# A hybrid encoder layer with the feed-forward layer's first product transposed: weights stationary, activations moving

## The chip, the cores and the metric

The kernel runs on one core of a Trainium2 chip. The metric is device time in microseconds for one execution; the figure is the median of several runs. The profile is one execution of its own, taken by the hardware profiler. The engines are PE (TensorE: matmuls; PEld is its loading of stationary operands), DVE (VectorE), ACT (ScalarE), POOL (GpSimd) and SP (SyncE, which issues the transfers).

## What is computed

One encoder layer with 256 rows (`S`), model width 2048 (`D`) and feed-forward width 8192 (`DFF`), in float32. The change touches the feed-forward part alone:

```python
# mod = silu(c) @ W_ada + b_ada -> shift, scale, gate of the mixer and of the FFN
h = modulate(rmsnorm(x, g_norm_ffn), shift_f, scale_f)     # (256, 2048)
f = jnp.square(jax.nn.relu(h @ w_ff1))                     # (256, 8192)
x = x + gate_f * (f @ w_ff2)                               # (256, 2048)
y = rmsnorm(x, g_final)
```

To keep float32 accuracy with the faster format fp32r, every operand is split into a rounded high part and the low remainder, and a product is the sum of three: high·high, activation high·weight low, activation low·weight high.

## The kernel before

The 256 rows are two token tiles (`T` = 2) of 128. A matmul takes a stationary operand of 128 × 128 and moves up to 512 columns past it, and its result stands in a PSUM bank of 128 × 512 floats. All big products go through `block` (L282): it fetches two k's (2 × 128 rows of weights, 1024 columns, 1 MB) at a time into a ring of `RAW_BUFS` = 5 raw tiles (DMA issued by SP), `split` (L120) casts each 128 × 1024 slice to the high part on ACT (L123) and subtracts on DVE for the low part (L124), with `W_BUFS` = 4 tiles of each. Then come the matmuls of L309: stationary is the activation slice of one k and one token tile, high or low; moving are 512 weight columns. A block of 1024 columns fills four banks, one for each token tile and column half, from the pool of four "mm" banks that all blocks share; the last two k's go token tile by token tile, and `evac` follows for each bank.

The feed-forward stage runs like this:

- `h2_first(t)` (L835) makes the modulated, normalised and transposed h of k 0 to 7 for one token tile: transposes (L858), modulation (L829, L831), high part on ACT (L863), low part on DVE (L864). `h2_first(0)` runs in the middle of the mixer's output product, `h2_first(1)` behind it.
- `ff1_first(ci)` (L904), for chunks 0 to 3 of 1024 hidden columns: the product over k 0 to 7, copied to `parts[ci]` (L906). Beside it the stream `ada_l` makes scale and shift of the FFN on DVE (L376; SP fetches 1 MB for every two of its steps). The first of these blocks takes the first 6 k's token tile by token tile (`HEAD` = 3), so that its 36 matmuls of tile 0 stand ahead of the first of tile 1.
- `h2_second` (L878), when `shift_f` is there and turned into columns by 16 matmuls (L417): h for k 8 to 15, with 16 transposes (L889), high part L892, low part L893.
- The main loop (L992): `ff1(ci)` (k 8 to 15 for the first four chunks, all 16 k's for the others), then `ff2(ci - 1)`, then `ff_T(ci)`. `ff1`'s `evac` adds the stored part on DVE, applies ReLU on ACT and squares on DVE into `rl`, which is token-major. `ff_T` (L929) turns it: 16 transposes of 128 × 128 in four banks, a copy to `fh` on ACT (L938), a subtraction to `fl` on DVE (L939). `ff2` (L942) is two blocks of 8 k's with `fh` and `fl` as stationary operands and `evac` into `acc` (L951 and on).

The order of instructions on each engine is a static list: the `run` calls interleave the generators, and a scheduler sets the list by the order and its own estimate of times. Each engine works through its list in order.

## Time and profile before

| | |
|---|---|
| median of 3 runs | 1185.48 us (1183.98 to 1187.21) |
| the profiled execution, its own time | 1184.91 us |
| its span in the trace | 1183.1 us |
| mean granted TensorE clock | 0.993 |
| PE busy | 1139.7 us, 96%, 5502 matmuls and transposes |
| DVE busy | 810.0 us, 68% |
| ACT busy | 552.4 us, 47% |
| moved by DMA | 297.50 MB, mean 251 GB/s |

The span runs from the first to the last instruction in the trace; the 1.8 us beside it are what the execution's own time has more. The feed-forward stage takes from about 448 us, the first `f1a` matmul, to the end. In rows of the timeline a line is a run of like instructions: its start, its time to the end of the last one, their number (x4), and in brackets how long the engine had been idle before and what released it. [...]

### The profile page before, as it was taken

What the parts mean: (1) busy time and instruction counts of PE and PEld (TensorE: products, weight loads), DVE (VectorE), ACT (ScalarE), POOL (GpSimd) and SP (SyncE); (2) the same over time, 40 slices, a digit from 0 to 9 for tenths busy, and PEclk for the clock granted to TensorE, in tenths of its full rate; (3) what the DMA queues carried; (4) which work ended last, traced back from release to release, by engine and by line L of the source; (5) the groups of instructions that cost most, each with busy time, mean ns of one, the idle gap of its engine ahead of it and who ended that gap; (6) DMA issues with size and microseconds to landing.
All of it is one profiled execution on the core that took longest, in us unless ns stands there. A gap on an engine that the chain in (4) does not pass through costs nothing.

```text
span 1183.1 us, 14211 instructions
## 1 busy us (share of the span) xinstructions
PE 1139.7 (96%) x5502; PEld 913.8 (77%) x5502; DVE 810.0 (68%) x1012; ACT 552.4 (47%) x811; POOL 53.3 (5%) x50
## 2 busy tenths in 40 slices
PE   5999999998999998999999999999999999999996
PEld 4566778865778886888888888888888888888875
DVE  3245559996899869775754666676686676555776
ACT  3432334547774436545545444344344344344343
POOL 1000000112101000000000000000020002000000
PEclk9999999999999999999999999999999999999999
DMA  9999974786788877995565646667868767556531
GB/s 347 393 390 369 359 302 131 258 308 215 294 307 300 300 276 275 356 329 194 184 225 179 204 158 207 232 236 263 278 220 277 280 241 249 183 181 203 183 104 72
DMA packets 94196, 297.50 MB, mean 251 GB/s; under 512 B 5712, under 2 KB 16167, under 8 KB 93488
## 3 DMA queue, kind: packets, MB, share of 16 engines
q1 hardware_dynamic: 94016, 296.56, 71.3%
q8 instruction: 43, 0.70, 0.2%
q14 instruction: 25, 0.20, 0.0%
q10 hardware_dynamic: 112, 0.03, 0.0%
HBM read 294.47 MB, written 2.10 MB: 251 GB/s over the span
## 4 chain that ended last, share of the span: by engine, by line
PE 59%; DVE 1%; issue 1%; ACT 0%; ACTq 0%; POOLq 0%; POOL 0%
PE f_p L309 51%; PE f1a_p L309 7%; PE fT L936 1%; DVE x_res L954 0%; DVE acc L953 0%; DVE acc L951 0%; PE shift_f_pc L417 0%; PE scale_f_pc L417 0%; PE h2T L889 0%; ACT acc L885 0%; DVE acc L957 0%; ACT sq L960 0%; PE h2a L858 0%; ACT h2a10t L831 0%; ACT acc L981 0%
## 5 line engine op out<-in xcount | busy, mean ns | idle before, releaser
L124 DVE TENSOR_TENSOR f_w_lo<-f_r,f_w_hi 128x1024 fp32r<-128x1024 f32 x224 | 277.2, 1245 | 200.9 <-ACT f_w_hi L123 200.8
L123 ACT CAST f_w_hi<-f_r 128x1024 fp32r<-128x1024 f32 x224 | 236.2, 1054 | 317.6 <-PE f_p L309 300.3
L309 PE MATMUL f_p<-f_w_hi,h 128*128 128x512 f32 x768 | 209.5, 391 | 0.0
L309 PEld LDWEIGHTS f_p<-f_w_hi,h 128*128 128x128 f32 x768 | 143.4, 188 | 29.3 <-ACT h L892 0.2
L309 PE MATMUL f_p<-f_w_lo,fh 128*128 128x512 f32 x512 | 158.9, 389 | 0.0
L309 PE MATMUL f_p<-f_w_hi,fh 128*128 128x512 f32 x512 | 158.5, 390 | 0.3 <-ACT fh L938 0.3
L309 PE MATMUL f_p<-f_w_hi,fl 128*128 128x512 f32 x512 | 158.7, 389 | 0.0
L309 PE MATMUL in_p<-in_w_hi,hT 128*128 128x512 f32 (+1 forms) x512 | 140.8, 388 | 4.6 <-ACT hT L364 2.8
L309 PE MATMUL f_p<-f_w_lo,h 128*128 128x512 f32 x384 | 118.9, 390 | 0.0
L309 PEld LDWEIGHTS in_p<-in_w_hi,hT 128*128 128x128 f32 x512 | 95.0, 189 | 29.0 <-ACT in_w_hi L123 6.3
L309 PEld LDWEIGHTS f_p<-f_w_hi,fh 128*128 128x128 f32 x512 | 96.0, 188 | 21.6 <-DVE acc L951 1.2
L309 PEld LDWEIGHTS f_p<-f_w_hi,fl 128*128 128x128 f32 x512 | 96.0, 188 | 20.0
L309 PEld LDWEIGHTS f_p<-f_w_lo,fh 128*128 128x128 f32 x512 | 96.1, 188 | 19.7
L124 DVE TENSOR_TENSOR in_w_lo<-in_r,in_w_hi 128x1024 fp32r<-128x1024 f32 (+1 forms) x64 | 73.2, 1169 | 45.1 <-ACT in_w_hi L123 44.9
L309 PEld LDWEIGHTS f_p<-f_w_lo,h 128*128 128x128 f32 x384 | 72.0, 188 | 14.8
L309 PE MATMUL in_p<-in_w_lo,hT 128*128 128x512 f32 (+1 forms) x256 | 78.8, 386 | 1.7 <-DVE in_w_lo L124 1.5
L123 ACT CAST in_w_hi<-in_r 128x1024 fp32r<-128x1024 f32 (+1 forms) x64 | 62.8, 1010 | 37.0 <-PE in_p L309 27.4
L309 PE MATMUL f1a_p<-f1a_w_hi,h 128*128 128x512 f32 x256 | 69.4, 391 | 3.0 <-ACT h L863 3.0
L309 PEld LDWEIGHTS f1a_p<-f1a_w_hi,h 128*128 128x128 f32 x256 | 47.8, 188 | 14.0 <-ACT h L863 3.9
L309 PEld LDWEIGHTS in_p<-in_w_lo,hT 128*128 128x128 f32 x256 | 47.7, 189 | 12.2 <-DVE in_w_lo L124 5.1
L123 ACT CAST out_w_hi<-out_r 128x1024 fp32r<-128x1024 f32 x30 | 31.6, 1052 | 35.7 <-PE out_p L309 35.7
L376 DVE SCALAR_TENSOR_TENSOR gate_f<-gate_f_r,cs,gate_f 128x1024 f32<-128x1024 f32 x32 | 40.9, 1280 | 7.0 <-DMA gate_f_r<-w_ada 6.9
(341 smaller groups left out, 1374.9 us busy)
## 6 DMA issues: line engine op xcount, KB each, us to landing
f_r<-w_ff SPq DMA_DIRECT2D x112, 1024.0 KB, 5.6
in_r<-w_in SPq DMA_DIRECT2D x24, 1024.0 KB, 9.9
sc__r<-w_ada SPq DMA_DIRECT2D x16, 1024.0 KB, 12.1
sh__r<-w_ada SPq DMA_DIRECT2D x16, 1024.0 KB, 13.4
gate_m_r<-w_ada SPq DMA_DIRECT2D x16, 1024.0 KB, 6.8
scale_f_r<-w_ada SPq DMA_DIRECT2D x16, 1024.0 KB, 8.0
...
```

What stands on the lines that cost most here:

```text
L123: s.copy(hi, src)
L124: v.tensor_tensor(lo, src, hi.bitcast(F32), ALU.subtract)
L309: pe.matmul(ps[t][j][:, 0:nw], lhsT=lhs[(lk0 + kk) // 8][:, (lk0 + kk) % 8, t * P:(t + 1) * P], rhs=rhs[:, n0:n0 + nw], start=(kk == 0 and ...
L376: v.scalar_tensor_tensor(acc, raw[:, i, :], cs[:, k + i:k + i + 1], acc, op0=ALU.mult, op1=ALU.add)
L936: pe.transpose(pt[:, i * S + t * P:i * S + (t + 1) * P], rl[:, t, (kp + i) * P:(kp + i + 1) * P], ident)
```

## The change

`ff1` is turned round. `ff1_block` (L901 to L944 of the new file) handles 512 hidden columns (`SC`; 16 blocks, numbered `si`) in four banks `u` of 128 hidden columns each. The stationary operand is now a 128 × 128 weight slice; moving are activations. h's high and low parts lie side by side in one tile (`both`), so a high weight goes against [h high | h low], 512 columns, and fills both halves of a bank; a low weight goes against h high, 256 columns, and adds to the left half. A raw tile holds four k's of 512 columns. The last four k's go bank by bank, each followed by its `evac`. The bank's two halves are then added: for `f1a` a copy of the left half on ACT and an addition on DVE into `parts`; for the first eight `ff1` blocks two DVE additions (stored part, then right half); for the other eight a copy on ACT and an addition. For each pair of banks a `scalar_tensor_tensor` on DVE takes max with 0 and multiplies by itself, ACT casts the high part of f and DVE subtracts for the low part, both straight into a tile `fs[si]`, hidden-major, as `ff2` needs it. `ff_T` goes.

The first `f1a` block (`by_tile`) loads all its weights, then takes the high weights against token tile 0 (32 matmuls of 2 × 128 columns), against token tile 1, and then the low weights against both tiles. `HEAD` goes from `block`.

`ff2(ci)` takes `fs[2ci]` and `fs[2ci + 1]`, uses other banks ("at" and "gv"), and comes after `ff1(2ci + 2)`, so one `ff1` block stands between it and the last f that it needs; the last `ff2` follows the last `ff1`. The gate's stream starts at `si` = 8. The other edits only lay out tiles.

```diff
-    def block(w_view, k0, nk, c0, w, lhs_hi, lhs_lo, name, evac, lk0=None, tail=1, rot=0, head=1, mid=None):
+    def block(w_view, k0, nk, c0, w, lhs_hi, lhs_lo, name, evac, lk0=None, tail=1, rot=0, mid=None, kdiv=8, tags=("mm",) * 4):
...
-                ps = [[bank(f"{name}_p{t}{j}", "mm") for j in range(2)] for t in range(T)]
+                ps = [[bank(f"{name}_p{t}{j}", tags[2 * t + j]) for j in range(2)] for t in range(T)]
...
-            if not last and (k + 2 + 2 * tail > nk or k + 2 < 2 * head):
+            if not last and k + 2 + 2 * tail > nk:
...
-            outer = last or k + 2 == 2 * head > 2
-            order = [(t, e) for t in range(T) for e in held] if outer else [(t, e) for e in held for t in range(T)]
+            order = [(t, e) for t in range(T) for e in held] if last else [(t, e) for e in held for t in range(T)]
...
-                pe.matmul(ps[t][j][:, 0:nw], lhsT=lhs[(lk0 + kk) // 8][:, (lk0 + kk) % 8, t * P:(t + 1) * P],
+                pe.matmul(ps[t][j][:, 0:nw], lhsT=lhs[(lk0 + kk) // kdiv][:, (lk0 + kk) % kdiv, t * P:(t + 1) * P],
...
-    def pair(name, halves, dt=F32R):
-        return [[act.tile([P, 8, S], dt, tag=f"h{hf}{part}", name=f"{name}{hf}{part}") for hf in halves]
-                for part in range(2)]
+    def both(name, hf):
+        return act.tile([P, 8, 2, S], F32R, tag=f"h{hf}", name=f"{name}{hf}")
+
+    def pair(name, halves):
+        tiles = [both(name, hf) for hf in halves]
+        return [[t_[:, :, part, :] for t_ in tiles] for part in range(2)]
...
-            v.tensor_tensor(h2_lo[0][:, 4 * q:4 * q + 4, tl], t3, hq.bitcast(F32), ALU.subtract)
+            v.tensor_tensor(h2[0][:, 4 * q:4 * q + 4, 1, tl], t3, hq.bitcast(F32), ALU.subtract)
...
-            s.copy(h2_hi[1][:, k - 8, :], tmp)
-            v.tensor_tensor(h2_lo[1][:, k - 8, :], tmp, h2_hi[1][:, k - 8, :].bitcast(F32), ALU.subtract)
+            s.copy(h2[1][:, k - 8, 0, :], tmp)
+            v.tensor_tensor(h2[1][:, k - 8, 1, :], tmp, h2[1][:, k - 8, 0, :].bitcast(F32), ALU.subtract)
...
+    SC = 512
+    NS = DFF // SC
+    NU = SC // P
+
+    def ff1_block(si, k0, nk, name, evac, by_tile=False):
+        ps, held = None, []
+        for k in range(0, nk, 4):
+            raw = raw_tile([P, 4, SC], f"{name}_r{k}")
+            sy.dma_start(raw, w_ff1_v[:, k0 + k:k0 + k + 4, si * SC:(si + 1) * SC])
+            for i in range(0, 4, 2):
+                hi, lo = split([P, 2, SC], raw[:, i:i + 2, :], f"{name}_w{k + i}")
+                held += [(k + i + j, hi[:, j, :], lo[:, j, :]) for j in range(2)]
+            if ps is None:
+                ps = [bank(f"{name}_p{u}", "mm") for u in range(NU)]
+            last = k + 4 >= nk
+            if by_tile and not last:
+                yield 0.0
+                continue
+
+            def mm(u, w, kk, o, h, start, stop):
+                pe.matmul(o, lhsT=w[:, u * P:(u + 1) * P], rhs=h, start=start, stop=stop)
+
+            def act_of(kk):
+                return h2[(k0 + kk) // 8][:, (k0 + kk) % 8]
+
+            if by_tile:
+                for t in range(T):
+                    tl = slice(t * P, (t + 1) * P)
+                    for u in range(NU):
+                        for kk, hi, lo in held:
+                            mm(u, hi, kk, ps[u].rearrange("p (a q) -> p a q", a=2)[:, :, tl], act_of(kk)[:, :, tl],
+                               t == 0 and kk == 0, False)
+                for u in range(NU):
+                    for kk, hi, lo in held:
+                        mm(u, lo, kk, ps[u][:, 0:S], act_of(kk)[:, 0, :], False, kk == nk - 1)
+                    evac(u, ps[u])
+            else:
+                order = [(u, e) for u in range(NU) for e in held] if last else [(u, e) for e in held for u in range(NU)]
+                for u, (kk, hi, lo) in order:
+                    h = act_of(kk)
+                    if kk == nk - 1:
+                        mm(u, lo, kk, ps[u][:, 0:S], h[:, 0, :], False, False)
+                        mm(u, hi, kk, ps[u], h.rearrange("p a q -> p (a q)"), False, True)
+                        evac(u, ps[u])
+                    else:
+                        mm(u, hi, kk, ps[u], h.rearrange("p a q -> p (a q)"), kk == 0, False)
+                        mm(u, lo, kk, ps[u][:, 0:S], h[:, 0, :], False, False)
+            yield 2.6 * len(held) * SC / 1024
+            held = []
+
+    def ff1_first(si):
+        def evac(u, ps):
+            part = parts[si // 2][:, si % 2 * NU + u, :]
+            s.copy(part, ps[:, 0:S])
+            v.tensor_tensor(part, ps[:, S:2 * S], part, ALU.add)
+
+        yield from ff1_block(si, 0, 8, f"f1a_{si}", evac, by_tile=si == 0)
+
+    fs = {}
+
+    def ff1(si):
+        split_k = si < 8
+        pool, tag = ((act, "n0"), (act, "n1"), (ff, "rl"))[si % 3]
+        f = fs[si] = pool.tile([P, 2, NU, S], F32R, tag=tag, name=f"f{si}")
+        box = []
+
+        def evac(u, ps):
+            if u % 2 == 0:
+                box[:] = [small.tile([P, 2, S], F32, tag="tmp", name=f"fr{si}{u}", bufs=2)]
+            tmp = box[0]
+            tu = tmp[:, u % 2, :]
             if split_k:
+                v.tensor_tensor(tu, ps[:, 0:S], parts[si // 2][:, si % 2 * NU + u, :], ALU.add)
             else:
+                s.copy(tu, ps[:, 0:S])
+            v.tensor_tensor(tu, ps[:, S:2 * S], tu, ALU.add)
+            if u % 2:
+                us = slice(u - 1, u + 1)
+                v.scalar_tensor_tensor(tmp, tmp, 0.0, tmp, op0=ALU.max, op1=ALU.mult)
+                s.copy(f[:, 0, us, :], tmp)
+                v.tensor_tensor(f[:, 1, us, :], tmp, f[:, 0, us, :].bitcast(F32), ALU.subtract)
 
         k0 = 8 if split_k else 0
+        yield from ff1_block(si, k0, KT - k0, f"f1_{si}", evac)
...
-    def ff2(ci, f_hi, f_lo, last):
+    def ff2(ci, last):
...
+            f_hi, f_lo = ([fs[2 * ci + i][:, part] for i in range(2)] for part in range(2))
...
+                             tail=TAIL[1] if last and n0 else 1, kdiv=NU, tags=("at", "at", "at", "gv"))
...
-    run((42.0, chain(*[ff1_first(ci) for ci in range(NSPLIT)])), (LW, ada_l))
+    run((42.0, chain(*[ff1_first(si) for si in range(8)])), (LW, ada_l))
     if late:
         run((1.0, flush()))
     h2_second()
-    pend = None
-    for ci in range(NCH + 1):
-        hold = []
-        if ci == NSPLIT and ada_f is None:
+    gate_f, ada_f = None, None
+    for si in range(NS + 1):
+        if si == 8:
             gate_f = act.tile([P, D], F32, tag="gate", name="gate_f")
             ada_f = chain(ada_gate(5, gate_f, "gate_f", late), flush())
-        na = 0 if ada_f is None or ci == 0 else 3 if NSPLIT == 4 else 2
-        if ci < NCH:
-            run((42.0, ff1(ci, hold)), (2.0, take(ada_f, na)))
-        if pend is not None:
-            last = ci == NCH
-            run((42.0, ff2(ci - 1, *pend, last)), (2.0, take(ada_f, na)))
-        if ci < NCH:
-            pend = ff_T(ci, hold[0])
-        if ci == 5:
+        if si < NS:
+            run((21.0, ff1(si)), (2.0, take(ada_f, 2 if ada_f else 0)))
+        if si >= 2 and si % 2 == 0:
+            run((42.0, ff2(si // 2 - 1, si == NS)), (2.0, take(ada_f, 3 if ada_f else 0)))
+        if si == 11:
             gfin = ff.tile([P, D], F32, tag="gfin", name="gfin")
             sy.dma_start(gfin, g_final.partition_broadcast(P))
 
```

PE, at the start of the first `f1a` block, before: `f1a_p` are banks, `h_3695` and `h_3696` the high and low part of h for k 0 to 7, `h2a` the transposes of token tile 1. The two rows of tile 0 with the transposes between them:

```order
L309 MATMUL f1a_p_3831<-f1a_w_hi,h_3695 128x512
L309 MATMUL f1a_p_3830<-f1a_w_lo,h_3695 128x512
L858 MATMUL h2a_3781<-ident,xs_3778 128x128 x4
L858 MATMUL h2a_3793<-ident,xs_3778 128x128 x4
L309 MATMUL f1a_p_3831<-f1a_w_lo,h_3695 128x512
L309 MATMUL f1a_p_3830<-f1a_w_hi,h_3696 128x512
```

Of the change, from the block's first matmul: four banks (3823 to 3826) of tile 0, eight k's each, high weights alone, then the transposes, then the same for tile 1, then the low weights.

```order
L917 MATMUL f1a_p_3823<-h_3690,f1a_w_hi 128x2x128 x4
L917 MATMUL f1a_p_3824<-h_3690,f1a_w_hi 128x2x128
L917 MATMUL f1a_p_3823<-h_3690,f1a_w_hi 128x2x128 x4
L917 MATMUL f1a_p_3824<-h_3690,f1a_w_hi 128x2x128 x7
L917 MATMUL f1a_p_3825<-h_3690,f1a_w_hi 128x2x128 x8
L917 MATMUL f1a_p_3826<-h_3690,f1a_w_hi 128x2x128 x8
L858 MATMUL h2a_3775<-ident,xs_3772 128x128 x4
L858 MATMUL h2a_3787<-ident,xs_3772 128x128 x4
L917 MATMUL f1a_p_3823<-h_3690,f1a_w_hi 128x2x128 x8
L917 MATMUL f1a_p_3824<-h_3690,f1a_w_hi 128x2x128 x8
L917 MATMUL f1a_p_3825<-h_3690,f1a_w_hi 128x2x128 x8
L917 MATMUL f1a_p_3826<-h_3690,f1a_w_hi 128x2x128 x8
```

The low weights have moved behind tile 1's matmuls, and 32 matmuls stand ahead of tile 1's.

DVE, where `h2_second` starts, before: `mf` are the modulation's columns, `h2t` the modulated h of one k, `h_3808` the low part of h for k 8 to 15.

```order
L423 COPY mf<-shift_f_pc 128x8
L829 TENSOR_SCALAR h2t_4477<-h2T_4474,mf 128x256
L124 TENSOR_TENSOR f_0_w_lo<-f_0_r_4568,f_0_w_hi 128x1024
L893 TENSOR_TENSOR h_3808<-h2t_4477,h_3807 128x256
L893 TENSOR_TENSOR h_3808<-h2t_4484,h_3807 128x256
L829 TENSOR_SCALAR h2t_4491<-h2T_4488,mf 128x256
L893 TENSOR_TENSOR h_3808<-h2t_4491,h_3807 128x256
L893 TENSOR_TENSOR h_3808<-h2t_4498,h_3807 128x256
```

Of the change, from the same copy; `part` and `f1a_p` belong to the last `f1a` block's `evac`, `f_0_w_lo` to the splits of the first `ff1` block.

```order
L421 COPY mf<-shift_f_pc 128x8
L123 TENSOR_TENSOR f_0_w_lo<-f_0_r_4796,f_0_w_hi 128x1024
L951 TENSOR_TENSOR part_3810<-f1a_p_4592,part_3810 128x256
L831 TENSOR_SCALAR h2t_4696<-h2T_4693,mf 128x256
L123 TENSOR_TENSOR f_0_w_lo<-f_0_r_4796,f_0_w_hi 128x1024
L891 TENSOR_TENSOR h_3801<-h2t_4696,h_3801 128x256
L891 TENSOR_TENSOR h_3801<-h2t_4703,h_3801 128x256
L831 TENSOR_SCALAR h2t_4710<-h2T_4707,mf 128x256
L891 TENSOR_TENSOR h_3801<-h2t_4710,h_3801 128x256
```

A split and an addition have moved between `mf` and the first modulation.

PE, at the boundary between two chunks before: the end of the first half of `ff2(0)`, `ff_T(1)`'s transposes and the start of `ff1(2)`.

```order
L309 MATMUL f_0_1024_p_5021<-f_0_1024_w_hi,fl_4683 128x512
L309 MATMUL f_0_1024_p_5022<-f_0_1024_w_hi,fl_4683 128x512
L936 MATMUL fT_0_5155<-ident,rl_4712 128x128 x4
L936 MATMUL fT_2_5162<-ident,rl_4712 128x128 x4
L936 MATMUL fT_4_5169<-ident,rl_4712 128x128 x4
L309 MATMUL f_2_p_5194<-f_2_w_hi,h_3807 128x512
L309 MATMUL f_2_p_5195<-f_2_w_hi,h_3807 128x512
L309 MATMUL f_2_p_5194<-f_2_w_lo,h_3807 128x512
L309 MATMUL f_2_p_5195<-f_2_w_lo,h_3807 128x512
L936 MATMUL fT_6_5176<-ident,rl_4712 128x128 x4
L309 MATMUL f_2_p_5194<-f_2_w_hi,h_3808 128x512
```

Of the change, between the first and second `ff1` block (`f_0`, `f_1`; banks 4760 to 4763 and 4865 to 4868):

```order
L917 MATMUL f_0_p_4763<-h_3801,f_0_w_lo 128x256
L917 MATMUL f_0_p_4763<-h_3801,f_0_w_hi 128x512
L917 MATMUL f_0_p_4763<-h_3801,f_0_w_lo 128x256 x2
L917 MATMUL f_0_p_4763<-h_3801,f_0_w_hi 128x512
L917 MATMUL f_1_p_4865<-h_3801,f_1_w_hi 128x512
L917 MATMUL f_1_p_4865<-h_3801,f_1_w_lo 128x256
L917 MATMUL f_1_p_4866<-h_3801,f_1_w_hi 128x512
L917 MATMUL f_1_p_4866<-h_3801,f_1_w_lo 128x256
L917 MATMUL f_1_p_4867<-h_3801,f_1_w_hi 128x512
L917 MATMUL f_1_p_4867<-h_3801,f_1_w_lo 128x256
```

The transposes are gone, and blocks follow each other directly; the new block's fourth bank comes 15 matmuls behind its first.

DVE there, of the change: the third and fourth bank's additions (L969, L972), the pair's square (L975) and low part (L977), and splits of the next weights.

```order
L969 TENSOR_TENSOR fr_4838<-f_0_p_4762,part_3807 128x256
L972 TENSOR_TENSOR fr_4838<-f_0_p_4762,fr_4838 128x256
L977 TENSOR_TENSOR f_4749<-fr_4814,f_4749 128x512
L969 TENSOR_TENSOR fr_4838<-f_0_p_4763,part_3807 128x256
L123 TENSOR_TENSOR f_1_w_lo<-f_1_r_4901,f_1_w_hi 128x1024
L972 TENSOR_TENSOR fr_4838<-f_0_p_4763,fr_4838 128x256
L123 TENSOR_TENSOR f_1_w_lo<-f_1_r_4901,f_1_w_hi 128x1024
L975 SCALAR_TENSOR_TENSOR fr_4838<-fr_4838 128x512
L123 TENSOR_TENSOR f_2_w_lo<-f_2_r_4960,f_2_w_hi 128x1024
L977 TENSOR_TENSOR f_4749<-fr_4838,f_4749 128x512
```

Now a split stands between the fourth bank's two additions (L969 and L972 of `f_0_p_4763`).

## Rows read from the trace of the kernel before

**Rows 1.** The page's part 1: busy time, share and instructions of each engine.

```profile
PE 1139.7 (96%) x5502; PEld 913.8 (77%) x5502; DVE 810.0 (68%) x1012; ACT 552.4 (47%) x811; POOL 53.3 (5%) x50
```

**Rows 2.** Windows: stretch, length, busy PE, PEld, DVE, ACT, POOL; clock, DMA share, GB/s.

```profile
460.00:543.00 83.00, 82.88 (x383) 69.25 (x384) 62.56 (x58) 40.38 (x48) 1.07 (x2) 1.00 0.91 333
767.00:855.00 88.00, 88.00 (x397) 72.70 (x396) 61.84 (x59) 37.87 (x40) 0.00 (x0) 1.00 0.76 263
```

**Rows 3.** Chain of waits, 855 to 952 us: start, length, work, one chunk of it.

```profile
858.17 1.31 PE fT L936 x12
859.49 1.61 PE f_p L309 x7
861.09 0.58 PE fT L936 x4
861.67 85.59 PE f_p L309 x377
```

**Rows 4.** Timeline of PE: first transpose of `ff_T`, one of its last, the last matmul.

```profile
567.04 0.49 PE L936 MATMUL fT<-ident,part 128*128 128x128 f32 x3
...
1130.45 0.66 PE L936 MATMUL fT<-ident,rl 128*128 128x128 f32 x4 [1.28 <-DVE fl L939]
...
1172.23 0.61 PE L309 MATMUL f_p<-f_w_hi,fl 128*128 128x512 f32 x2
```

**Rows 5.** Timeline of PE, 770 to 790 us: `ff1` over all k's.

```profile
774.51 1.07 PE L309 MATMUL f_p<-f_w_hi,h 128*128 128x512 f32 x4
...
788.11 1.07 PE L309 MATMUL f_p<-f_w_hi,h 128*128 128x512 f32 x4
```

**Rows 6.** Timeline of PE around 325 and 229 us: matmuls of 256 columns.

```profile
324.46 0.40 PE L552 MATMUL pq<-cq,q_hi 128*128 128x256 f32 x2
...
326.62 0.40 PE L552 MATMUL pq<-cq,q_hi 128*128 128x256 f32 x2
...
228.71 0.28 PE L552 MATMUL pv<-kv_hi,cq 128*128 128x256 f32 x1
228.83 0.63 PE L309 MATMUL in_p<-in_w_hi,hT 128*128 128x512 f32 x2
```

**Rows 7.** Timeline of PE, 438 to 464 us: the first `f1a` block.

```profile
448.12 0.73 PE L309 MATMUL f1a_p<-f1a_w_hi,h 128*128 128x512 f32 x2 [1.59 <-ACT h L863]
...
455.57 1.06 PE L858 MATMUL h2a<-ident,xs 128*128 128x128 f32 x8 [0.27 <-DVE xs L850]
...
460.12 0.73 PE L309 MATMUL f1a_p<-f1a_w_hi,h 128*128 128x512 f32 x2 [1.43 <-ACT h L863]
```

**Rows 8.** Timeline of DVE there: the low part of h, token tile 1.

```profile
460.15 0.68 DVE L864 TENSOR_TENSOR h<-h2a10t,h 128x512 fp32r<-128x512 f32 x1
```

**Rows 9.** Timeline of all engines, 540 to 546 us: `h2_second`.

```profile
540.98 1.84 PE L417 MATMUL shift_f_pc<-ones,shift_f 128*128 128x1 f32 x16
...
542.86 0.17 DVE L423 COPY mf<-shift_f_pc 128x8 f32<-128x8 f32 x1 [0.73 <-PE shift_f_pc L417]
...
544.17 0.74 PE L309 MATMUL f_p<-f_w_hi,h 128*128 128x512 f32 x2
```

**Rows 10.** Timeline of PE at 372 us, and windows behind it as in rows 2.

```profile
372.38 1.84 PE L417 MATMUL scale_f_pc<-ones,scale_f 128*128 128x1 f32 x16
...
375.50:376.00 0.50, 0.31 (x2) 0.31 (x3) 0.50 (x3) 0.50 (x1) 0.00 (x0) 0.50 0.96 385
378.50:379.00 0.50, 0.50 (x3) 0.40 (x2) 0.50 (x2) 0.00 (x0) 0.00 (x0) 0.62 1.01 401
```

**Rows 11.** Groups by line and shape: count, busy us, mean ns; idle before.

```profile
L124 DVE TENSOR_TENSOR f_w_lo<-f_r,f_w_hi 128x1024 fp32r<-128x1024 f32 x224 | 277.2, 1245 | 200.9 <-ACT f_w_hi L123 200.8
L123 ACT CAST f_w_hi<-f_r 128x1024 fp32r<-128x1024 f32 x224 | 236.2, 1054 | 317.6 <-PE f_p L309 300.3
L951 DVE TENSOR_TENSOR acc<-f_p,acc 128x512 f32<-128x512 f32 x48 | 30.8, 683 | 1.8 <-PE f_p L309 1.8
L893 DVE TENSOR_TENSOR h<-h2t,h 128x256 fp32r<-128x256 f32 x8 | 3.0, 418 | 0.5 <-ACT h L892 0.5
```

More of the change, by code (lines that the diff above doesn't have):

```diff
@@ L776, in encoder_layer @@
         (RW[7], take(ada_m, NA_[2])))
-    asc = [act.tile([P, D], F32, tag=f"h1{i}", name=f"asc{i}") for i in range(2)]
+    asc_t = act.tile([P, 2 * D], F32, tag="h1", name="asc")
+    asc = [asc_t[:, i * D:(i + 1) * D] for i in range(2)]
     p_ring = [asc[i // 4][:, i % 4 * 512:(i % 4 + 1) * 512].rearrange("p (a q) -> p a q", a=2) for i in range(6)]
@@ L869, in encoder_layer @@
     mix_stack.close()
[L872 to L874 removed]
+    h2.append(both("h2", 1))
     ff = ctx.enter_context(tc.tile_pool(name="ff", bufs=1))
@@ L891, in h2_second @@
             mod(tmp, pt[:, 0:S], k)
-            s.copy(h2_hi[1][:, k - 8, :], tmp)
-            v.tensor_tensor(h2_lo[1][:, k - 8, :], tmp, h2_hi[1][:, k - 8, :].bitcast(F32), ALU.subtract)
+            s.copy(h2[1][:, k - 8, 0, :], tmp)
+            v.tensor_tensor(h2[1][:, k - 8, 1, :], tmp, h2[1][:, k - 8, 0, :].bitcast(F32), ALU.subtract)
     FC = 1024
     NCH = DFF // FC
-    gate_f = None
-    if NSPLIT < 4:
-        gate_f = act.tile([P, D], F32, tag="gate", name="gate_f")
-    parts = [ff.tile([P, T, FC], F32, tag=("rl", "gfin", "part")[i], name=f"part{i}") if i < 3 else
-             act.tile([P, T, FC], F32, tag="gate", name=f"part{i}") for i in range(NSPLIT)]
@@ L902, in encoder_layer @@
-    ada_f = None if gate_f is None else chain(ada_gate(5, gate_f, "gate_f", late), flush())
-    def ff1_first(ci):
-        def evac(t, j, o, w, ps):
-            s.copy(parts[ci][:, t, o:o + w], ps)
-        yield from block(w_ff1_v, 0, 8, ci * FC, FC, h2_hi, h2_lo, f"f1a_{ci}", evac,
-                         head=HEAD if ci == 0 else 1)
-    def ff1(ci, hold):
-        split_k = ci < NSPLIT
-        rl = parts[0] if ci == 0 and split_k else ff.tile([P, T, FC], F32, tag="rl", name=f"rl{ci}")
-        def evac(t, j, o, w, ps):
-            dst = rl[:, t, o:o + w]
+    parts = [ff.tile([P, 8, S], F32, tag=("rl", "gfin", "part")[i], name=f"part{i}") if i < 3 else
+             act.tile([P, 8, S], F32, tag="gate", name=f"part{i}") for i in range(4)]
@@ L917, in evac @@
             if split_k:
-                part = parts[ci][:, t, o:o + w]
-                v.tensor_tensor(part, ps, part, ALU.add)
-                s.activation(dst, part, AF.Relu)
-            else:
-                s.activation(dst, ps, AF.Relu)
-            v.tensor_tensor(dst, dst, dst, ALU.mult)
-        k0 = 8 if split_k else 0
-        yield from block(w_ff1_v, k0, KT - k0, ci * FC, FC, h2_hi, h2_lo, f"f1_{ci}", evac)
-        hold.append(rl)
-    def ff_T(ci, rl):
-        f_hi = act.tile([P, FC // P, S], F32R, tag="n0", name=f"fh{ci}")
-        f_lo = act.tile([P, FC // P, S], F32R, tag="n1", name=f"fl{ci}")
-        for kp in range(0, FC // P, 2):
-            pt = bank(f"fT{ci}_{kp}")
-            for i in range(2):
-                for t in range(T):
-                    pe.transpose(pt[:, i * S + t * P:i * S + (t + 1) * P], rl[:, t, (kp + i) * P:(kp + i + 1) * P], ident)
-            p3 = pt.rearrange("p (k q) -> p k q", k=2)
-            s.copy(f_hi[:, kp:kp + 2, :], p3)
-            v.tensor_tensor(f_lo[:, kp:kp + 2, :], p3, f_hi[:, kp:kp + 2, :].bitcast(F32), ALU.subtract)
-        return [f_hi], [f_lo]
```

13 lines of the change are left out of this document (3 added, 10 removed).

## The prediction

> **What bounds the kernel now.** I read the totals first. PE (TensorE, the matrix engine) is busy 96% of the span and DVE (VectorE) 68% [rows 1]. Then I looked at the two stretches that the change rewrites, by the windows: in the feed-forward stage PE is busy 82.88 of 83.00 us before the second half of h exists, and 88.00 of 88.00 us after it, at a granted clock of 1.00; DVE has about a quarter to a third of each stretch free [rows 2]. So here nothing is gained by shortening a transfer or a DVE instruction. Only PE's own list of work counts, with the few places where it stands still. The chain of waits says the same: through a whole chunk it is product matmuls and the transposes of `ff_T`, nothing else [rows 3]. A chunk therefore costs (number of matmuls) × (their spacing) + transposes + waits, and the change touches all three.
>
> **Spacing, the unit of the sum.** [...] Between the two rows of [rows 5] lie 60 matmuls with 512 columns: 13.60 us, 226.7 ns each. Between the first two of [rows 6] lie 18 with 256 columns: 2.16 us, 120 ns each. Both carry one weight load per matmul. [...] A crossing from 256 to 512 columns costs nothing more: 0.12 us from the short one's start to the long one's (the last two lines of [rows 6]).
>
> **The terms**, against the profiled execution's own 1184.9 us (0.6 below the median of the three, 1185.5).
>
> 1. *`ff_T` goes.* From the first transpose at 567.04 to the last matmul's issue, half a microsecond behind 1172.23 [rows 4], are 605.65 us. In it stand 2592 matmuls of 512 columns (1056 of `ff1`, 1536 of `ff2`), 587.5 us. The rest, 18.1 us, is transposes and waits for `ff_T`. One chunk bears it out: 1.31 + 0.58 us of transposes and 0.16 us more around 384 matmuls [rows 3], and eight chunks give 16.4; the last adds waits such as the 1.28 us for `fl` [rows 4]. The new code writes f hidden-major, ready as ff2's stationary operand, and `ff2` runs one `ff1` block later, so nothing waits for the last f but the last ff2: its f needs an add, a multiply, a cast and a subtraction behind the last `ff1` matmul, and that is covered because ff2's first k's use the other f tiles. **−18.1.**
>
> 2. *The first product's matmuls.* Before: three of 512 columns per token tile, k and column half, 1536 × 0.2267 = 348.2 us. After: a high weight times [h high | h low] (512) and a low weight times h high (256): the same columns in more instructions. 992 of 512 and 1088 of 256 (the first block splits the wide one by token tile): 224.9 + 130.6 = 355.4 us. **+7.3**, of which 2.1 in the early blocks.
>
> 3. *Less cover in the first block.* Before, PE starts on token tile 0 at 448.12, when h high is written, and has 36 long matmuls (8.2 us) to do until tile 1's h comes at 460.12 [rows 7]. After, PE has 32 short ones (3.84 us), because low weights wait until both tiles are through. They also need h low, which DVE starts at 460.15 for tile 1 [rows 8], 0.7 us behind the high part. 8.16 − 3.84 = 4.3, and a little for h low: **+4.5** (4.3 to 5.0).
>
> 4. *`h2_second`.* Before, from the start of `shift_f_pc` at 540.98 [rows 9] to 567.04 are 26.06 us for 96 matmuls (21.8): 4.3 us go to other things. After, DVE's order puts a low split and an add ahead of the first h (order section). From the copy `mf` at 542.86 [rows 9]: split 1.2, add 0.4, modulation 0.5, split 1.2, subtraction 0.4 [rows 11], so the first matmul stands some 5.7 us behind the start, plus 0.6 of later transposes: 6.3. **+2.0** (0 to 3).
>
> 5. *The clock.* [...] Two falls of 1.7 us: **+3.4**; at worst a few us, at best 0, as [rows 9] before show matmuls at full pace behind a gap of 3 us.
>
> 6. *New waits for banks.* Before, four "mm" banks were freed by ACT (ScalarE) copies. Now each bank of a split-k block needs two DVE additions, with DVE's splits queued between. PE asks for the fourth bank 2.65 us after a block's start (8 × 0.2267 + 7 × 0.12). **+1.5** (0 to 12).
>
> Taken at nothing: two transfers' worth of 2 KB instead of 4 KB rows (the DMA engines are at 0.91 in the tight stretch [rows 2], and five raw buffers stand ahead); `ff2`'s banks, now its own; the multiply, cast and subtraction that make f, on engines that have room [rows 2]. If that cover goes, it is rival A.
>
> Sum: −18.1 + 7.3 + 4.5 + 2.0 + 3.4 + 1.5 = +0.6, so **1185.5 us**: no change. The terms' own bounds make 1182 to 1189 of it.
>
> [...]
>
> **Rivals.**
>
> *A, slower: DVE paces the split-k blocks.* A block has 11.09 us of PE work (32 × 0.2267 + 32 × 0.12). DVE has four splits at 1.245, eight additions of 256 at 0.418 and four 512-wide operations at 0.683 [rows 11]: 11.0 us by these means, some 10.1 where they run back to back. That is 91 to 99% of the block, in a fixed order in which a split that waits for ACT's cast (1.05) stands between the fourth bank's two additions (order section). It decides where the second addition ends later than 2.65 us behind the block's start. Add 0.4, a split of 1.2 with its wait for the cast, add 0.4, all behind a queue of some 1.5: about 3.5 to 4. Then each of eight blocks loses about 1.2 us: +10 over the 1.5 already in, less what overlaps, so **1194**. Against: the additions of the earlier banks fall within the block. Chance 0.27.
>
> *B, faster: the clock stays and no bank is late.* −3.4 − 1.5: **1180.6**. For: in the 83 us of [rows 2] PE hardly ever stood. Against: [rows 10]. Chance 0.20.
>
> [...] Chance 0.10. [...]
>
> *D, the weight load sets the pace.* PEld (the weight loads) has 913.8 us for 5502 loads, 166 ns each [rows 1], more than a short matmul's 120. Were a short one never faster than that, 1088 × 0.046 = 50 us would be added: **1235**. [Rows 6] exclude it as far as they reach. Chance 0.03.
>
> **How the numbers follow.** A measurement here can tell about 0.3%, 3.6 us, from no change: 1181.9 to 1189.0. The forecast has 0.40. Faster takes B less its upper edge, and C: 0.28. Slower takes A and D and the forecast's upper edge: 0.32. Cases of both signs hold more than half; the forecast's own range is 1182 to 1189. For 8 in 10 I go from C's 1179.5 to A's 1194; outside lie D, a worse A, and several gains at once.
>
> **What would show it.** Right: no PE transposes inside the feed-forward chunks; 512- and 256-column matmuls in alternation at 0.227 and 0.120 us; a first block with a hole of some 7 us in PE before tile 1's h; a gap of 5 to 6 us at `shift_f_pc`; windows with clock below 1.00 behind these two. Rival A: PE idle before the fourth bank of the split-k blocks, released by DVE's second addition, and DVE near 100% there. B: clock 1.00 throughout. [...] The prediction falls if pairs cost far more than 0.347 us, or if the split-k stage runs over 11.5 us a block.

## The result and the profile after

The changed kernel takes 1198.26 us (median of four runs, 1197.20 to 1201.66), the kernel before 1185.88 us beside it: a ratio of 1.0111, with an interval of 1.0095 to 1.0127. It is slower by 12.4 us, where no change was forecast. The profiled execution took 1197.79 us; its span is 1196.0 us, 12.9 above that of before, and this difference is accounted for below.

The page's part 1 after, against [rows 1]: PE has 4.5 us more busy time and 416 more instructions (544 matmuls more, 128 transposes fewer), DVE 39 us more.

```profile
PE 1144.2 (96%) x5918; PEld 930.9 (78%) x5918; DVE 849.2 (71%) x1124; ACT 546.4 (46%) x827; POOL 52.5 (4%) x50
```

The timeline of PE, start of the feed-forward stage (start, duration, work, number, idle time before and its releaser), against [rows 7]. From the first `f1a` matmul to token tile 1's first are 12.49 us, with 4.66 us of work (32 matmuls at 0.12 and eight transposes, 0.82 at the full clock); before they were 12.00 us with 8.98 of work. Tile 1's 32 matmuls are then listed with 5.80 us where tile 0's have 4.10. A matmul is listed with more time than passes until the next one starts, 0.28 us against 0.12 in [rows 6], so spacings are read from start to start.

```profile
446.86 4.10 PE L917 MATMUL f1a_p<-h,f1a_w_hi 128*128 128x256 f32 x32 [2.29 <-DVE h L864]
453.21 1.94 PE L858 MATMUL h2a<-ident,xs 128*128 128x128 f32 x8 [2.25 <-DVE xs L850]
459.35 5.80 PE L917 MATMUL f1a_p<-h,f1a_w_hi 128*128 128x256 f32 x32 [4.20 <-DVE h L864]
464.99 4.00 PE L917 MATMUL f1a_p<-h,f1a_w_lo 128*128 128x256 f32 x32
```

The windows say why (columns as in [rows 2]; the granted clock is third from the end). Behind the idle 2.25 us the clock is at 0.50 until 463.2, and again for 3.4 us behind `h2_second`; in the windows that follow it is at 1.00.

```profile
453.00:463.10 10.10, 5.69 (x25) 5.32 (x26) 7.09 (x12) 4.11 (x9) 0.00 (x0) 0.50 0.88 295
463.30:466.00 2.70, 2.70 (x25) 2.70 (x24) 2.23 (x2) 1.53 (x2) 0.00 (x0) 1.00 0.00 0
555.50:558.70 3.20, 3.20 (x13) 2.82 (x12) 1.93 (x6) 2.33 (x6) 0.00 (x0) 0.50 0.83 242
560.00:565.00 5.00, 5.00 (x31) 4.34 (x30) 2.72 (x4) 3.28 (x5) 0.00 (x0) 1.00 0.01 3
```

The first of these two falls also delays h, because the transposes that h waits for run at half clock. In the profile of the first experiment below the clock fell only after them; there they are listed with 1.06 us instead of 1.94, and tile 1 starts 11.72 us behind the block's start instead of 12.49. The profiles of the changed kernel and of its variants below, but for the one with filler matmuls, divide in this way: seven with the transposes at the full clock have 11.72 or 11.73 us, four with them at half, this one among them, have 12.48 to 12.50.

```profile
448.77 4.09 PE L918 MATMUL f1a_p<-h,f1a_w_hi 128*128 128x256 f32 x32 [2.29 <-DVE h L864]
455.12 1.06 PE L858 MATMUL h2a<-ident,xs 128*128 128x128 f32 x8 [2.26 <-DVE xs L850]
460.49 5.79 PE L918 MATMUL f1a_p<-h,f1a_w_hi 128*128 128x256 f32 x32 [4.30 <-DVE h L864]
```

`h2_second` in the timeline of PE and of DVE, against [rows 9]: the column sums, then DVE's list in the predicted order, a split and an addition ahead of the first modulation, and the first product matmul 5.49 us behind the start.

```profile
549.61 1.84 PE L415 MATMUL shift_f_pc<-ones,shift_f 128*128 128x1 f32 x16
...
551.49 0.17 DVE L421 COPY mf<-shift_f_pc 128x8 f32<-128x8 f32 x1 [2.26 <-PE shift_f_pc L415]
551.57 1.22 DVE L123 TENSOR_TENSOR f_w_lo<-f_r,f_w_hi 128x1024 fp32r<-128x1024 f32 x1
552.71 0.42 DVE L951 TENSOR_TENSOR part<-f1a_p,part 128x256 f32<-128x256 f32 x1
553.05 0.53 DVE L831 TENSOR_SCALAR h2t<-h2T,mf 128x256 f32<-128x256 f32 x1
...
555.10 0.59 PE L917 MATMUL f_p<-h,f_w_hi 128*128 128x512 f32 x1 [1.03 <-DVE h L891]
```

In the rest of the stage the list of PE's waits (total, times, longest, 560 to 1190 us) has one line. None of its five waits lies in the split-k blocks (the first eight, which add a stored part). They stand at the start of the eleventh `ff1` block, at 869.67 and 872.53 us, and of the thirteenth, from 960.37 to 965.91. Taken from start to start, with the matmuls right beside them, they cost 6.2 us and not only the 4.6 of idle time. Before, the same list has no wait for a bank: 1.3 us for `fl` [rows 4] and 0.3 for `fh`.

```profile
PE f_p L917 <- DVE fr L972: 4.6, 5, 2.1
```

The rows of POOL and DVE around them show what DVE was doing. POOL adds up the gate over the partitions, two reductions of 3.2 to 4.1 us each time. Weight splits (L123) that start while they run take 3.2 to 3.3 us where [rows 11] have 1.2, and the square (L975) takes 2.31 us instead of 0.69. The bank additions (L972), with one operand in PSUM, still take 0.41 us, but queue behind. DVE has not caught up when the eleventh block starts at 868.61, 5.6 us behind the reductions: the addition at 872.06, for which PE waits until 872.53, stands behind a split that had itself waited for ACT's cast.

```profile
855.73 4.05 POOL L401 PARTITION_ALL_REDUCE gate_f<-gate_f  x1 [303.26 <-issue]
859.69 3.32 POOL L401 PARTITION_ALL_REDUCE gate_f<-gate_f  x1
956.66 6.45 POOL L401 PARTITION_ALL_REDUCE gate_f<-gate_f  x2 [93.65 <-DVE gate_f L374]
...
856.58 3.27 DVE L123 TENSOR_TENSOR f_w_lo<-f_r,f_w_hi 128x1024 fp32r<-128x1024 f32 x1
859.77 3.33 DVE L123 TENSOR_TENSOR f_w_lo<-f_r,f_w_hi 128x1024 fp32r<-128x1024 f32 x1
...
870.91 1.23 DVE L123 TENSOR_TENSOR f_w_lo<-f_r,f_w_hi 128x1024 fp32r<-128x1024 f32 x1 [0.26 <-ACT f_w_hi L122]
872.06 0.42 DVE L972 TENSOR_TENSOR fr<-f_p,fr 128x256 f32<-128x256 f32 x1
...
956.82 3.16 DVE L123 TENSOR_TENSOR f_w_lo<-f_r,f_w_hi 128x1024 fp32r<-128x1024 f32 x1
959.90 0.41 DVE L972 TENSOR_TENSOR fr<-f_p,fr 128x256 f32<-128x256 f32 x1
960.35 2.31 DVE L975 SCALAR_TENSOR_TENSOR fr<-fr 128x512 f32<-128x512 f32 x1
```

The kernel before had the same stretching, and PE waited for none of it: the banks of its `ff1` there were freed by ACT.

```profile
868.10 7.18 POOL L403 PARTITION_ALL_REDUCE gate_f<-gate_f  x2 [324.27 <-DVE gate_f L376]
...
869.40 7.10 DVE L124 TENSOR_TENSOR f_w_lo<-f_r,f_w_hi 128x1024 fp32r<-128x1024 f32 x3 [0.47 <-ACT f_w_hi L123]
```

The ends of the two engines' rows belong together. The split at 856.58 ends at 859.85 and the reduction at 859.78; the next pair ends at 863.10 and 863.01. In all the traces together 43 splits start inside one of the gate's reductions, 0.1 to 2.4 us behind its start; every one ends 0.07 to 0.09 us behind the reduction's end. The only other one starts 2.8 us behind the start and takes its own 1.21 us. Nine instructions of half the width (eight squares and one low part of f) end 0.44 to 0.45 us ahead of the reduction's end. Less their own 1.22 and 0.69 us, both widths come to the same moment, some 1.14 us before that end: they look as if they were held until then and ran at their own pace from there. The instructions that are hit (L123, L975 and the low part of f) have both inputs in SBUF; the additions of L972, which aren't (0.41 us at 959.90, inside the reductions), have one in PSUM. What holds them isn't shown. The other way round, the 13 reductions that start while a split runs take 3.95 to 4.14 us, the other 39 take 3.23 to 3.32.

Last, spacing. Two stretches of the timeline of PE hold the same alternation of 512 and 256 columns. Between the first two rows lie 12 pairs: 4.24 us, 353 ns each. Between the next two lie 21 pairs: 7.28 us, 347 ns each, which is the forecast (226.7 + 120). Both spacings are steady. The 14th `ff1` block has 353 ns through its first 48 pairs; the 15th changes to 347 right behind a single gap of 33 ns, at 1055.71 us.

```profile
864.13 0.28 PE L917 MATMUL f_p<-h,f_w_lo 128*128 128x256 f32 x1
...
868.37 0.28 PE L917 MATMUL f_p<-h,f_w_lo 128*128 128x256 f32 x1
...
1056.52 0.28 PE L917 MATMUL f_p<-h,f_w_lo 128*128 128x256 f32 x1
...
1063.80 0.28 PE L917 MATMUL f_p<-h,f_w_lo 128*128 128x256 f32 x1
```

In `ff2`, matmuls that take their stationary operand from the f tile in the buffer `rl` are 36 in 8.40 us, 233.3 ns each; with the other two f tiles they stand at 226.7.

```profile
658.13 1.09 PE L307 MATMUL f_p<-f_w_hi,f 128*128 128x512 f32 x4
...
666.53 1.09 PE L307 MATMUL f_p<-f_w_hi,f 128*128 128x512 f32 x4
```

### The profile page after: what moved, and what is told of

The parts are those of the page before. It is cut to its first block, busy times and chain, and to the rows that moved or that the text cites. A ratio compares the mean times of both kernels' runs of the same rounds, so it can differ in the third digit from the quotient of the medians.

```text
span 1196.0 us, 15207 instructions
## 1 busy us (share of the span) xinstructions
PE 1144.2 (96%) x5918; PEld 930.9 (78%) x5918; DVE 849.2 (71%) x1124; ACT 546.4 (46%) x827; POOL 52.5 (4%) x50
## 5 line engine op out<-in xcount | busy, mean ns | idle before, releaser
L123 DVE TENSOR_TENSOR f_w_lo<-f_r,f_w_hi 128x1024 fp32r<-128x1024 f32 x224 | 278.5, 1250 | 168.4 <-ACT f_w_hi L122 168.0
L307 PE MATMUL f_p<-f_w_hi,f 128*128 128x512 f32 x1024 | 278.6, 391 | 0.0
L917 PE MATMUL f_p<-h,f_w_hi 128*128 128x512 f32 x768 | 268.4, 399 | 5.7 <-DVE fr L972 4.6
L307 PEld LDWEIGHTS f_p<-f_w_hi,f 128*128 128x128 f32 x1024 | 192.2, 188 | 42.8 <-DVE acc L991 0.7
L917 PE MATMUL f_p<-h,f_w_lo 128*128 128x256 f32 x768 | 204.2, 281 | 0.0
L917 PEld LDWEIGHTS f_p<-h,f_w_hi 128*128 128x128 f32 x768 | 140.6, 189 | 36.4 <-DVE fr L972 6.5
L307 PE MATMUL f_p<-f_w_lo,f 128*128 128x512 f32 x512 | 159.9, 391 | 0.0
L917 PEld LDWEIGHTS f_p<-h,f_w_lo 128*128 128x128 f32 x768 | 145.4, 189 | 6.4
L307 PEld LDWEIGHTS f_p<-f_w_lo,f 128*128 128x128 f32 x512 | 96.1, 188 | 20.9
L123 DVE TENSOR_TENSOR in_w_lo<-in_r,in_w_hi 128x1024 fp32r<-128x1024 f32 (+1 forms) x64 | 73.2, 1169 | 43.9 <-ACT in_w_hi L122 43.7
L917 PE MATMUL f1a_p<-h,f1a_w_hi 128*128 128x512 f32 (+1 forms) x288 | 86.7, 381 | 6.5 <-DVE h L864 6.5
L917 PE MATMUL f1a_p<-h,f1a_w_lo 128*128 128x256 f32 x256 | 61.6, 281 | 0.0
L307 PEld LDWEIGHTS in_p<-in_w_lo,hT 128*128 128x128 f32 x256 | 47.8, 190 | 12.4 <-DVE in_w_lo L123 5.2
```

The source lines that it names most:

```text
L123: v.tensor_tensor(lo, src, hi.bitcast(F32), ALU.subtract)
L307: pe.matmul(ps[t][j][:, 0:nw], lhsT=lhs[(lk0 + kk) // kdiv][:, (lk0 + kk) % kdiv, t * P:(t + 1) * P], rhs=rhs[:, n0:n0 + nw], start=(kk == ...
L917: pe.matmul(o, lhsT=w[:, u * P:(u + 1) * P], rhs=h, start=start, stop=stop)
```

## The experiments

Each kernel is the changed one with the edit shown, except where stated. Places in SBUF are those of the compiled program, in bytes per partition.

**The place of the slow f tile.** Three kernels move the tile `rl`. After, it lies at byte 203,008; the other two f tiles lie at 145,088 and 153,280.

```diff
+    ff.tile([P, 16], F32, name="pad")      # first kernel: rl at 203,072
+    part0 = ff.tile([P, 8, S], F32, tag="rl", name="part0")   # second: ahead of acc, at 186,624
+    ff.tile([P, 368], F32, name="pad")     # third: at 204,480
     acc = [ff.tile([P, D], F32, name=f"acc{t}") for t in range(T)]
...
```

> One unused tile of 64 bytes ahead of the accumulators moves acc, the parts and the third f tile (tag rl) up by 64 bytes, so that rl starts at the same remainder of 128 bytes as every other operand; nothing else changes. In the changed kernel the ff2 matmuls whose stationary operand lies in rl stand 233.3 ns apart, those in n0 and n1 226.7. If the remainder of the address is what costs the 6.6 ns, the rl matmuls go to 226.7 ns, the five slow ff2 blocks pairs fall from 44.2 to 43.6 us and the kernel gains about 3.2 us. If it is the region of the memory, or something that goes on at the time, they stay at 233.3 and the time stays at 1198.

> The third f tile (tag rl, also the first part) is allocated ahead of the two accumulators, so it lies at byte 186,624 of each partition instead of 203,008; the accumulators move up. Where the tile starts modulo 128 is as in the changed kernel. If the region in which the stationary operand lies sets the spacing, the ff2 matmuls with that tile go from 233.3 to 226.7 ns and five of the eight ff2 fall from 44.2 to 43.6 us (3 us in all). If it hangs on something else of this tile (its turn, its neighbours in time, how it is written), they stay at 233.3 ns and the time at 1198.

> An unused tile of 1,472 bytes moves the third f tile so that it starts at the same remainder of 2,048 bytes (1,728) as the other two f tiles, the weights and h; in the changed kernel, with 64 bytes and in the other region its remainders were 256, 320 and 256. If the stationary operand's place relative to the moving one's in a block of up to 2,048 bytes sets the spacing, the matmuls with it go from 233.3 to 226.7 ns and the kernel gains about 3 us. If not, they stay at 233.3 ns and the time at 1198.

Measured: 1198.54 us (ratio 1.0119, 1.0103 to 1.0136), 1200.60 (1.0136, 1.0122 to 1.0150) and 1197.92 (1.0116, 1.0095 to 1.0136). In the first two the `rl` matmuls stay at 233.3 ns. In the third, the timeline of PE has 36 in 8.16 us, 226.7 ns:

```profile
658.11 1.07 PE L307 MATMUL f_p<-f_w_hi,f 128*128 128x512 f32 x4
...
666.27 1.07 PE L307 MATMUL f_p<-f_w_hi,f 128*128 128x512 f32 x4
```

So the place of the tile costs the 6.6 ns. Another region (186,624) stays slow, and so does a step of 64 bytes (203,072); a step of 1,472 bytes (204,480) doesn't. What it is about the place isn't shown by these; the remainders by which the first and the third were chosen were the author's guess. The repair is worth some 3 us in the trace, which the median of four runs doesn't resolve.

**What makes the pairs slip.** Either the stationary operand's new role or the mixture of widths. One kernel moves 512 columns for the low weights too, in the 5th and 14th `ff1` block (it adds low·low to the product there); one keeps the mixture and sends four wide, then four narrow.

```diff
+                if name in ("f1_4", "f1_13"):
+                    mm(u, lo, kk, ps[u], h.rearrange("p a q -> p (a q)"), False, False)
```

```diff
-                order = [(u, e) for u in range(NU) for e in held] if last else [(u, e) for e in held for u in range(NU)]
...
+                    for e in held:
+                        for u in range(NU):
+                            wide(u, e)
+                        for u in range(NU):
+                            thin(u, e)
```

> In the fifth and fourteenth ff1 block the low weights go against h high and h low, 512 columns, so that all their matmuls are wide (the low times low product is added; 192 matmuls of 256 columns become 512, some 20.5 us more). Theory that it is the alternation with narrow matmuls that costs 351 to 353 ns a pair: these two blocks run at 226.7 ns a matmul (14.5 and 58.0 us with an unbroken PE for 64 and 256), as the kernel before did. Rival that weights as stationary operands are loaded more slowly from where they lie: 230 to 234 ns (14.8 and 59.3 us or more).

> ff1's matmuls in groups: for each k the four of 512 columns, then the four of 256 (in the last k's three wide, four narrow, one wide for each bank), the same instructions as before in another order. Theory that wide and narrow in alternation cost 351 to 353 ns a pair instead of 347 because a narrow one leaves its neighbour's weight load too little room: the spacing goes to 226.7 and 120 ns, ff1 without waits falls by about 4 us (44.95 to 44.4 for 256 matmuls), the kernel gains 3 to 5 us. Rival that the extra belongs to weights as stationary operands or to what runs beside: 16 bank groups keep 351 to 353 ns a pair and the time stays within 1.5 us.

The first, with some 20 us of added work, took 1210.21 us in its one run, and in its 14th block 96 matmuls lie between the two rows of the timeline of PE, in 21.77 us, 226.8 ns each:

```profile
1036.95 0.40 PE L917 MATMUL f_p<-h,f_w_hi 128*128 128x512 f32 x1
...
1058.72 0.39 PE L917 MATMUL f_p<-h,f_w_hi 128*128 128x512 f32 x1
```

In its 5th block the change comes at once: the pairs before 645.92 us stand at some 353 ns, the wide matmuls from 646.39 on at 226.7. With weights stationary and one width there is no slip; it belongs to the mixture. It is the wide ones that slip, and they need no narrow neighbour for it: with grouping in fours a pair of blocks lasts 22.38 us instead of 22.53 (22.19 at 226.7 and 120 ns), its narrow matmuls stand at 118 ns and its wide ones, also those ahead of another wide one, at 232. So the forecast gain of 3 to 5 us did not come: about 1 us in all in the trace, and a median of 1200.00 (1.0123, 1.0106 to 1.0140).

**The waits behind the gate.** In the first kernel the gate's stream is taken only beside `ff2`. In the second the reduction is left out: ACT copies stand in for it, so the gate lacks its sum over the partitions.

```diff
-            run((21.0, ff1(si)), (2.0, take(ada_f, 2 if ada_f else 0)))
+            run((21.0, ff1(si)), (2.0, take(ada_f, 0)))
...
-            run((42.0, ff2(si // 2 - 1, si == NS)), (2.0, take(ada_f, 3 if ada_f else 0)))
+            run((42.0, ff2(si // 2 - 1, si == NS)), (2.0, take(ada_f, 6 if ada_f else 0)))
```

```diff
-                g.partition_all_reduce(gate[:, half * 1024 + j * 512:half * 1024 + (j + 1) * 512],
-                                       acc[:, j * 512:(j + 1) * 512], P, ReduceOp.add)
+                if which == 5:
+                    s.copy(gs, acc[:, j * 512:(j + 1) * 512])
```

> The gate's stream takes its 16 steps beside ff2 blocks only (6 at a time, none beside ff1), so that POOL's two pairs of partition reductions fall into ff2(4) and ff2(5) instead of the ends of the ninth and eleventh ff1 blocks. If POOL's reductions, which stretch DVE's instructions beside them from 1.22 to 2.2 us and more, are what made the banks late there, PE's 5.4 us of waits on the second addition go, and the kernel gains 4 to 5.5 us. If DVE is simply too full in these blocks (rival A of the prediction), the waits stay, at these places or at the split-k blocks, and the time changes by less than 1.5 us.

> The gate's sum over the 128 partitions is left out (POOL's four reductions become four copies on ACT, so the gate is wrong by that sum); the gate's stream on DVE and its transfers stay where they were. Theory that POOL's reductions stretch the DVE instructions beside them and so make the banks late: the 5.4 us of PE's waits on the second addition fall below 1 us, DVE's splits in these stretches last 1.22 us again, the kernel gains 4 to 5.5 us. Rival that the stream's own steps on DVE (1.28 us each, and their waits for transfers) do it: the waits stay at 3 us or more, the gain is below 2 us.

The first took 1194.08 us (1.0070, 1.0058 to 1.0082). Its `ff1` waits are gone, and the unsplit pairs of blocks are all alike at 44.94 to 44.96 us, where two of the changed kernel's have 47.32 and 49.16. What is left are short waits in `ff2`:

```profile
PE f_p L307 <- DVE acc L991: 0.8, 2, 0.5
```

The second took 1195.73 us (1.0096, 1.0080 to 1.0111). DVE's splits at the same place are back at 1.22 us, and of the waits 1.3 us are left, behind the gate's own multiplications:

```profile
856.37 1.22 DVE L123 TENSOR_TENSOR f_w_lo<-f_r,f_w_hi 128x1024 fp32r<-128x1024 f32 x1
...
PE f_p L920 <- DVE fr L975: 1.3, 2, 0.8
```

The two pairs of blocks last 45.64 and 46.27 us here. So POOL's reductions cause most of the new waits, by way of DVE; the gate's work on DVE causes the rest.

**The first block and `h2_second`.** The low weights go token tile by token tile, so that more work stands ahead of tile 1; and `h2_second` is given a higher priority in the scheduler, in the changed kernel and, in a third, in the kernel before.

```diff
+                    if t == 0:
+                        for u in range(NU):
+                            for kk, hi, lo in held:
+                                mm(u, lo, kk, ps[u][:, tl], act_of(kk)[:, 0, tl], False, False)
...
-    h2_second()
+    with tc.high_priority(offset=400):
+        if late:
+            run((1.0, flush()))
+        h2_second()
```

> In the first f1a block the low weights go against each token tile by itself, so 32 matmuls of 128 columns (about 2.1 us) are added to the cover ahead of token tile 1; the same work behind it falls to 32 of 128 columns. Theory that the hole ahead of token tile 1 and the fall of the clock behind it cost 7 us: the hole shrinks by 2 us, the clock's 10 us at half shorten or go, and the kernel gains 1.5 to 3.5 us. Rival that this stage is held by the arrival of h, and the matmuls behind it are paid anyway: gain below 0.7 us, as the extra instructions cost 0.5 us.

> The columns of shift_f and h2_second are given priority over the last two f1a blocks, so the h of k 8 to 15 is made while PE still has f1a matmuls. The 6.3 us around h2_second (0.8 of it matmuls that overlap nothing) and the fall of the clock behind it (1.8 us) should go, and the transposes stand between f1a matmuls: gain 4 to 8 us, with the window behind the first ff1 block at clock 1.00. Rival: shift_f's stream is bound by its transfers, PE and DVE then wait for it earlier in their lists and the gain is below 2 us, or it is slower.

> The kernel before with h2_second given priority over the last f1a block, and nothing else: it tells how much of that gain belongs to the change. The 4.3 us of other work at this place in the kernel before should shrink to the transposes' own 1.8 us and less: gain 2 to 4 us, 1181 to 1183. Rival: shift_f comes too late and PE waits for it: no gain or slower.

The first brought nothing: 1202.51 us (1.0147, 1.0124 to 1.0170; six runs from 1197.05 to 1206.76). Its tile 1 starts 11.72 us behind the block's start, as in every profile in which the transposes run at the full clock, so the 0.8 us to the changed kernel's 12.49 aren't the cover's: the arrival of h sets that start, not the work ahead of it.

```profile
447.98 5.47 PE L917 MATMUL f1a_p<-h,f1a_w_hi 128*128 128x256 f32 x32 [2.29 <-DVE h L864]
...
459.70 1.34 PE L917 MATMUL f1a_p<-h,f1a_w_hi 128*128 128x256 f32 x8 [1.79 <-DVE h L864]
```

The second shortens the stretch from the first `f1a` matmul to the first `ff2` from 144.3 to 139.1 us and has no fall of the clock at `h2_second`, but its median is only 1.1 us lower, 1197.17 (1.0101, 1.0084 to 1.0118). In its profile the waits around 960 us grow, with a fall of the clock of 6.8 us there, and the two pairs of blocks with the gate's waits take 1.0 us more; and its stage starts 2.8 us later (449.66), where nothing was edited. The kernel before gains nothing by it: 1184.34 (0.9998, 0.9987 to 1.0008).

**All repairs together.** The gate's place, the groups of four, the priority and the moved tile; then the same with 52 matmuls of 256 columns into an unread bank while PE waits for tile 1 (17 ahead of its transposes, 35 behind).

```diff
+                    if t == 0:
+                        fill = bank("fill", "gv")
+                        for i in range(52):
+                            kk, hi, lo = held[i % len(held)]
+                            mm(i % NU, hi, kk, fill[:, 0:S].rearrange("p (a q) -> p a q", a=2), act_of(kk)[:, :, tl],
+                               i == 0, i == 51)
```

> The gate's stream beside ff2 only, h2_second ahead of the last f1a blocks, ff1's matmuls in groups, and the third f tile at the others' remainder. If the causes are separate, their single gains add up: 4.2 for the gate, 5.2 for h2_second (of its own stretch), 1 for the groups and, if the place of the tile is a cause, 3 for it: 1185 us, or 1188 without the last. If they share one cause (DVE being late), the sum falls short by 4 us or more.

> The kernel with all four edits, and in its first f1a block 52 matmuls of 256 columns into a bank that nobody reads, 17 of them ahead of token tile 1's transposes and 35 behind: PE works through the time in which it has waited for h, and nothing else changes (the extra product is thrown away). Theory that part of this hole's price is the clock, which was granted at half in two stretches of 3.4 us around it (10 us in the changed kernel): the clock stays at full speed there, token tile 1 starts no later, the matmuls behind it go at 120 ns, gain 1.5 to 3.5 us on 1186.4. Rival that the hole costs only by waiting for h: no gain, or a loss of up to 1 us where the extra matmuls are in the way.

The first took 1186.38 us (12 runs; 1.0011, 0.9998 to 1.0025), 11.9 below the change alone, though its parts by themselves lowered the medians by 4.2 (gate), 1.1 (priority) and 0.3 (tile), and the groups of four raised it by 1.7, which is within their scatter. In the traces the sum comes out: in the stretches where they act they save 5.3, 5.2, 3.0 and 1.0 us, 14.5 together, and the stage, from the first `f1a` matmul to the end, falls from 749.1 to 734.7 (735.0 before the change). Why the single medians show so little of it is settled only in part: one profile each has the stage at 744.2, 746.1, 746.4 and 747.7, 12.0 us of savings, and the work ahead of it ends anywhere from 446.4 to 449.7 us without an edit there. With the filler: 1184.19 us (12 runs; 0.9991, 0.9978 to 1.0003). The intervals of the two ratios overlap, so a gain in the whole time isn't shown. The windows of both, the first without:

```profile
452.00:462.00 10.00, 4.92 (x30) 4.51 (x29) 9.56 (x15) 6.00 (x15) 1.41 (x1) 0.84 0.74 218
```

```profile
450.00:462.00 12.00, 11.39 (x92) 11.02 (x92) 11.56 (x18) 6.36 (x16) 1.40 (x1) 1.00 0.72 239
```

The clock stays at 1.00, while all eleven profiles of the changed kernel and its other variants have it at 0.50 for 6.8 to 10.2 us at this place. Tile 1 starts no later (11.71 us behind the block's start, 11.72 without), and its 32 matmuls take 3.94 us instead of 5.24. The repaired change equals the kernel before; nothing tried is shown to beat both.

## Why the prediction was wrong

Spans, term by term:

| term | predicted | measured |
|---|---|---|
| 1 `ff_T` goes | −18.1 | −18.1 |
| 2 number of matmuls | +7.3 | +7.3 |
| 2 their spacing | 0 | +8.7 |
| 3 less cover | +4.5 | +4.0 |
| 4 `h2_second` | +2.0 | +1.8 |
| 5 the clock | +3.4 | +4.3 |
| 6 waits for banks | +1.5 | +6.2 |
| work ahead of the stage | 0 | −1.3 |
| sum | +0.6 | +12.9 |

All are read from start to start in the two traces. Term 3 is (12.49 − 4.66) less (12.00 − 8.98), 4.8 us, of which 0.8 belongs to the clock. Term 4 is the 9.84 us from the start of `shift_f_pc` to 559.45, less 12 product matmuls (2.1), the clock (1.7) and the 4.3 of before.

Terms 1 and 3 to 5 held, in place and mechanism: no transposes in the chunks, a hole in the first block, 5.49 us at `shift_f_pc` where 5.7 was forecast, and two falls of the clock. Term 5's 1.7 us for each fall was the author's estimate. Before, the trace has one at 375 us: 0.96 in the window below and 0.62 in the second of [rows 10] put the clock at 0.50 from 375.46 to 378.88 us, 3.4 us; half of it is the 1.7.

```profile
375.00:375.50 0.50, 0.15 (x2) 0.00 (x0) 0.50 (x2) 0.50 (x2) 0.23 (x1) 0.96 0.79 270
```

After, the first fall lasted 10.2 us instead of 3.4 and cost 1.8 us in tile 1's matmuls and 0.8 in the transposes, which the prediction did not count; the second lasted 3.4 and cost 1.7.

**Term 2 failed in its spacing.** It carried the 226.7 and 120 ns of [rows 5, 6] over to a stream where both widths alternate and one operand lies elsewhere; [rows 6] had a single crossing, from which "costs nothing more" was read. The mixture cost 1.1 us in `f1a` (446 matmuls in 78.61 us instead of 77.20, less 0.3 of such gaps before; 0.5 of it is six short gaps) and 3.8 in `ff1`; the tile `rl` cost most of 3.8 in `ff2` (five of eight passes at 44.2 to 44.3 us instead of 43.5 to 43.6). The first is shown by the all-wide block, the second by the moved tile. The range had no bound for either.

**Term 6 failed in size and place.** Five waits cost 6.2 us against 1.5. The term looked for them in the split-k blocks, and rival A made its 1194 of the same place; no wait stands there. The shape of 872.53 is A's, an addition behind a split that waits for ACT's cast, but in a block without a stored part, and only while the gate keeps DVE late: with the gate beside `ff2` it is gone. They stand where POOL's reductions stretch DVE, now that a bank is free only after a DVE addition. The stretching was in the trace of before, but off PE's path, and the prediction never read POOL beside DVE: A's sum took 1.245 us for every split (and comes to 11.06 us, not 11.0, which changes nothing).

Rivals B and D fell, and so did the 1179.5 and the chance of 0.10 that stand for C: the clock did fall to 0.50, pairs stood 347 or 353 ns apart and not closer, and short matmuls ran at 120 ns under a weight load each.

Two things stay open. The pairs run at 347 or at 353 ns, and beyond the change behind one short gap nothing was found that decides. And in the first block PE waits for h, which no experiment brought forward by more than the clock's 0.8 us; why the totals of the kernel with more cover scatter by 10 us isn't known either.
